# Gated projection of a hybrid decoder trunk: the values of two column slices by seven block products as well, and the gates' weight sums by adding loads

## The chip, the cores and the metric

The kernel runs on one core of one Trainium2 chip. The metric is the device time of one execution, in microseconds (us); the kernel before takes 1935.12 us in the median of three runs (1935.08 to 1935.7). One execution was profiled. In it TensorE (PE) multiplies, VectorE (DVE) and ScalarE (ACT) prepare operands, GpSimd (POOL) and SyncE (SP) issue loads, each on a queue of its own, and 16 DMA engines move the data.

## The reference

A trunk of four residual layers on 256 tokens of width 2048, all float32: a convolution module, a dense MLP, a state-space layer, a dense MLP, then a norm. The change touches the end of the state-space layer, its gated projection:

```
y = jax.nn.gelu(y)                 # (256, 2048)
z = y @ w_glu                      # w_glu: (2048, 4096)
val, gate = jnp.split(z, 2, axis=-1)
x = x + val * jax.nn.sigmoid(gate)
```

Then the next MLP begins: `h = rms_norm(x, mlp_norm[1])`, `a = relu(h @ w_up)`, and so on. All weights come from HBM in float32, and each is used once.

## The kernel before

**Steps and halves.** The program is a list of steps (`self.steps`). A step is 1 MB of weights, 512 rows by 512 columns, which arrives in two halves of 512 KB, tiles of 128x1024. `run_steps` walks through the halves: it loads some steps ahead, splits some halves ahead, and multiplies. A plain step's halves are loaded by SP (`fetch`, L103) into one of six `raw` buffers.

**The split.** float32 is multiplied in three passes. `split` copies a half to a rounded tile `hi` on ACT (L156) and puts the remainder into `lo` on DVE (L163). There are four `hi` and four `lo` buffers, so a half can be split only when PE has done the half four places before it.

**A plain entry.** `mm_t` (L268 to L270) multiplies each half with 12 matmuls of 512 columns: two blocks of 128 rows, two blocks of 128 tokens, three passes. A plain entry is thus 24 matmuls. The activations are `yT`, the transposed output of the state-space part, made in four groups B = 0 to 3 of 512 rows each.

**The projection** (`glu`, from L1578). The outputs are four column slices n of 512 columns, each with values (h = 0) and gates (h = 1). For n = 0 and 1 the rows of groups 0 and 1 are multiplied first, by plain entries, and the partial sums are kept in `st["p"]`, named `part` in the profile. Slice n = 2 follows. Groups 2 and 3 of slices 0 and 1 are then added: the gates by `seven`, the values by four plain entries. Slice 3 is spread among these and ends the stage. While the first entries run, the last groups of the state-space part are finished at set places (`todo`), and loads of its tables (`Wt`, `Mt`, `Vt`) go out on SP's queue.

**Seven products** (`seven`, L745). A 2x2 block of weights B(r, c) (row parity r, column slice c) times a 2x2 block of activations is formed with seven block products instead of eight. A product is 12 matmuls (L759 to L761, accumulators `mp`, `mq`, `mr`), half a plain entry for PE, but it has two halves to split like one. The products' weights are, in order: 1: B(0,0); 2: X = B(0,0)+B(0,1); 3: B(1,1); 4: X, to which B(1,1) has been added; 5: Y = B(0,1)+B(1,1); 6: B(1,0); 7: X, to which B(1,0) has been added too. After each product `take` adds or subtracts the accumulator to one or two 128x512 blocks of `part` on DVE. The combined activations stand in the tile `F`, formed by `forms(2)` and `forms(3)`.

**Two ways to sum weights.** `also` lets DVE add a raw half to a tile `sum` (after `lo`, in `split`). A chain (`add_chain`) loads on POOL's queue: a plain load into `sum` (L129), or an adding load that adds the HBM data to what the tile holds (L123). Tiles `sum` come from a pool of six 512 KB buffers (tag `t4`), shared with temporaries of the stage. Before the change X is summed by DVE and Y, and X's last term, by adding loads.

**What sets the order.** The steps' order is written out by hand at the end of `glu`. Within it a scheduler places the instructions on each engine; every engine and every queue then works in its order.

Of the kernel before, what the change touches and what calls it, by code (L numbers as in the profile page):

```python
# [14 lines left out]
ALU = mybir.AluOpType  # L15
# [6 lines left out]
D = 2048  # L22
# [9 lines left out]
NQ = 4  # L32
# [5 lines left out]
class Trunk:  # L38
# [66 lines left out]
    def load(self, i, half=None):  # L105
        view, shape, _, pre = self.steps[i]
        for kind in self.before_load.pop(i, ()):
            self.table(*kind)
        self.loaded = i + 1
        chain = None  # L110
        if view is None:
            return
        if pre == "x":
            chain, shape = shape, [P, 4, 512]
            if i >= self.widen_from and self.wide is None:
                self.widen()
        nk = shape[1] // 2
        for hf in (0, 1) if half is None else (half,):
            k = slice(hf * nk, hf * nk + nk)
            size = [P, nk] + list(shape[2:])  # L120
            if chain is not None:
                if hf in chain:
                    self.nc.gpsimd.dma_start(out=chain[hf], in_=view[:, k], accum_op=ALU.add)  # L123
                    continue
                raw = chain[hf] = self.sum_tile(size)
            else:
                raw = self.raws[2 * i + hf] = self.w.tile(size, F32, tag="raw", name="raw", bufs=6)
            if chain is not None:
                self.nc.gpsimd.dma_start(out=raw, in_=view[:, k])  # L129
            elif len(shape) == 4:  # L130
                for j in range(shape[2]):
                    self.fetch(raw[:, :, j, :], view[:, k, j, :])
            else:
                self.fetch(raw, view[:, k])
# [607 lines left out]
            self.after(4, lambda: self.square_rstd(ssq))  # L742


    def seven(self, B, A, take, done, start):  # L745

        acc = {}

        def part(i, form, bank, first, *takes):
            def consume(hi, lo, half):
                start()
                if first and half == 0:
                    acc[bank] = self.bank([P, 512], name="m" + bank)
                mm = partial(self.nc.tensor.matmul, acc[bank], skip_group_check=True)
                for j in range(2):
                    F = [A(form, half, j, low) for low in range(2)]
                    mm(lhsT=F[0], rhs=hi[:, j, :], start=first and half == j == 0, stop=False)  # L759
                    mm(lhsT=F[0], rhs=lo[:, j, :], start=False, stop=False)  # L760
                    self.mm_last = mm(lhsT=F[1], rhs=hi[:, j, :], start=False, stop=half == j == 1)  # L761
                if half == 1:
                    with self.tc.high_priority(offset=URGENT):
                        for c, b, sub in takes:
                            take(c, b, sub, acc[bank])
                    if i in done:
                        done[i]()
            return consume
        A11, A22, A12, S1, S2, S3, S4 = range(1, 8)
        add, sub = 0, 1  # L770
        X, Y = {}, {}
        load = self.add_chain

        def plain(b, c, *sums):
            if sums:
                self.also[len(self.steps)] = sums
            self.add(b, [P, 4, 512], c)
        return [lambda: load(B(0, 1), Y),
                lambda: plain(B(0, 0), part(1, A11, "p", True, (0, 0, add)), X, Y),
                lambda: load(None, X, part(2, S1, "r", True, (1, 1, sub))),  # L780
                lambda: plain(B(1, 1), part(3, S4, "r", False, (1, 0, sub)), X, None),
                lambda: load(None, X, part(4, S2, "p", False, (1, 0, sub))),
                lambda: load(B(1, 1), Y, part(5, S3, "p", False, (1, 1, sub))),
                lambda: plain(B(1, 0), part(6, A12, "q", True, (0, 0, add))),
                lambda: load(B(1, 0), X, part(7, A22, "p", False, (0, 1, add)))]

    def mlp(self, layer, last_slice, last_block, hooks=None):
# [131 lines left out]
        if layer == 0:  # L919
# [18 lines left out]
            return down(nsl - 1)  # L938
        self.widen_from = len(self.steps)
        m = [[seven(s, n) for n in (0, 2)] for s in range(nsl)]  # L940
        for k in range(7):
            up(0, k)
# [635 lines left out]
    def glu(self):  # L1578
        w = self.a["ssm_w_glu"][0]
        st = {}  # L1580
# [56 lines left out]
        def out(B):  # L1637
            with self.behind(self.mm_last):
                self.ssm_out(B)
            return self.yt  # L1640

        def local(B):
            with self.behind(self.mm_last):
                self.ssm_local(B)
            return self.mmm

        def carry(B):
            with self.behind(self.mm_last):
                self.ssm_carry(B)
            return self.vmm  # L1650
# [14 lines left out]
        def scale3():  # L1665
            with self.behind(self.lo_ins):
# [5 lines left out]
                (5, 0): (lambda: local(2), scale3), (6, 0): (lambda: front(3),),  # L1672
                (6, 1): (lambda: turn(3), lambda: scan(3)), (7, 1): (lambda: forth(3),), (8, 1): (lambda: states(3),),
                (7, 0): (lambda: carry(2),), (8, 0): (lambda: out(2),), (9, 0): (lambda: local(3),),
                (11, 0): (lambda: carry(3),), (12, 0): (lambda: out(3),), (13, 0): (lambda: forms(2),),
                (13, 1): (lambda: forms(3),)}
        self.before_load = {len(self.steps) + i: t for i, t in ((6, (("W", 3),)), (7, (("M", 2), ("R", 3))), (10, (("V", 2),)),
                                                                (11, (("M", 3),)), (14, (("V", 3),)))}
        self.barrier = len(self.steps)

        order = [(n, B) for n in (0, 1) for B in (0, 1)] + [(2, B) for B in range(NQ)]
        order += [(n, B) for n in (0, 1) for B in (2, 3)] + [(3, B) for B in range(NQ)]

        def forms(B):

# [18 lines left out]
            b, m = ((0, 0), (1, 1), (0, 1))[i - 1]  # L1704
            return self.yT[1][:, 4 * half + 2 * j + m, low, b * P:(b + 1) * P]

        def gates():

            v = w[D // 2:].rearrange("(k two p) c -> two p k c", two=2, p=P)

            def take(c, b, sub, acc):
                c = st["p"][:, c, 1, b]
                self.tt(c, acc, c, ALU.add) if not sub else self.tt(c, c, acc, ALU.subtract)

            def done(n):
                self.nc.scalar.activation(st["p"][:, n, 1], st["p"][:, n, 1], AF.Sigmoid)
                self.glu_out(n, st["p"][:, n, 0], st["p"][:, n, 1])
                self.feed(n, st["ssq"], "mlp1")
            return self.seven(lambda r, c: v[r, :, :, D + c * 512:D + (c + 1) * 512], side, take,
                              {5: lambda: done(1), 7: lambda: done(0)}, lambda: None)  # L1720
        plain = []
        for i, (n, B) in enumerate(order):
            for h in (1, 0):
                def consume(hi, lo, half, n=n, B=B, h=h, i=2 * i + 1 - h):
                    ins = None
                    for fn in todo.pop((i, half), ()):
                        ins = fn() or ins
                    if i == half == 0:
                        st["ssq"] = self.new_ssq()
                    two = n < 2  # L1730
                    first = (B == 0 or two and B == 2) and half == 0
                    last = (B == NQ - 1 or two and B == 1) and half == 1
                    if first:
                        st[h] = self.acc2()
                    k0 = (B % 2) * 4 + half * 2
                    with self.behind(ins) if ins is not None else nullcontext():
                        self.mm_t(st[h], lambda kk: self.yT[B // 2][:, k0 + kk], hi, lo, first, last)
                    if not last:
                        return
                    if B == 1:  # L1740
                        if n == 0 and h == 1:
                            st["p"] = self.blk_tile([P, 2, 2, NB, 512], name="part")
                        self.nc.scalar.activation(st["p"][:, n, h], st[h], AF.Copy)
                    elif two:
                        self.tt(st["p"][:, n, 0], st[0], st["p"][:, n, 0], ALU.add)
                    elif h == 1:
                        st["g"] = self.t4([P, NB, 512], name="sg")
                        self.nc.scalar.activation(st["g"], st[1], AF.Sigmoid)
                    else:
                        if n == 2:  # L1750
                            self.new_hT()
                        self.glu_out(n, st[0], st["g"])
                        self.feed(n, st["ssq"], "mlp1")
                plain.append(partial(self.add_t, w, B * 4, h * D + n * 512, consume, begin if i == 0 and h == 1 else None))
        g = gates()
        a, p = plain[17:24:2], plain[24:]
        for e in (*plain[:15], g[0], plain[15], g[1], a[0], g[2], a[1], g[3], a[2], g[4], a[3], g[5], p[0], g[6], p[1], g[7],
                  *p[2:]):
            e()

    def glu_out(self, n, val, g):
# [97 lines left out]
```

## Time and profile before

| | |
|---|---|
| median of three runs | 1935.12 us (1935.08 to 1935.7) |
| the profiled execution's own time | 1935.06 us |
| its span in the profile | 1933.3 us |
| granted TensorE clock, mean | 0.999 |
| PE busy | 1915.5 us, 99% of the span |
| DVE / ACT / POOL busy | 86% / 58% / 20% |
| DMA | 468 MB, mean 242 GB/s |

Times of the trace are in us from the span's start. The projection's first matmul with `yT` starts at 1060.7, its last product of the gates ends at about 1223, and the next MLP's first matmuls start at 1256. Busy times of an engine add up the durations of its instructions that overlap at their ends, so the pace of an engine is read from the starts of successive instructions. "Landing" of a load is counted from its issue.

### The profile page before, as it was taken

The page shows a single profiled execution, that of the slowest core. Times are in us where ns is not written, and L with a number is a line of the kernel's source. Part 1 is how long each engine was busy: PE and PEld are TensorE (multiplying, and loading weights), DVE is VectorE, ACT ScalarE, POOL GpSimd, SP SyncE. Part 2 cuts the span into 40 slices and gives each one's busy share as a digit, 9 for nine tenths or more (in the row PEclk, how much of TensorE's full clock was granted, in tenths as well). Part 3 has the DMA queues.
Part 4 walks back from the last instruction along what each step waited for, and adds up shares of the span by engine and source line. Part 5 has one row for each costly group of instructions (what it writes and reads, how often), then busy time and mean ns, then how long its engine had stood idle before and what let it go on. Part 6 is the DMA issues. An engine that isn't in the chain of part 4 may idle for free.

```text
span 1933.3 us, 30420 instructions
## 1 busy us (share of the span) xinstructions
PE 1915.5 (99%) x11372; PEld 1641.5 (85%) x11372; DVE 1656.2 (86%) x2246; ACT 1124.9 (58%) x1405; POOL 395.6 (20%) x364
## 2 busy tenths in 40 slices
PE   8999999999999999999999999999999999999998
PEld 8999788888888888888888788888888888888887
DVE  6999798899878898988557869679999999999987
ACT  6444555554465565655545446566666666667664
POOL 3899300001021221213101001001111111111100
PEclk9999999999999999999999999999999999999999
DMA  9667468778788888888898978668998998989984
GB/s 247 186 183 217 124 209 251 220 243 270 251 205 251 238 289 233 280 225 278 280 339 302 337 247 219 195 208 229 260 265 228 266 265 239 260 252 254 247 258 145
DMA packets 338675, 468.45 MB, mean 242 GB/s; under 512 B 16801, under 2 KB 218593, under 8 KB 335169
## 3 DMA queue, kind: packets, MB, share of 16 engines
q1 hardware_dynamic: 296464, 364.69, 59.1%
q0 software_dynamic: 38496, 97.27, 21.5%
q10 hardware_dynamic: 3568, 4.56, 0.8%
q8 instruction: 89, 1.46, 0.3%
q14 instruction: 58, 0.48, 0.1%
HBM read 439.93 MB, written 34.91 MB: 246 GB/s over the span
## 4 chain that ended last, share of the span: by engine, by line
PE 96%; DVE 2%; DMA 1%; issue 0%; ACT 0%; POOL 0%; SPq 0%; POOLq 0%; DVEq 0%; ACTq 0%
PE acc L245 24%; PE acc L248 13%; PE acc L268 7%; PE acc L269 7%; PE acc L270 7%; PE mp L760 4%; PE mp L761 4%; PE mp L759 4%; PE acc L257 3%; PE acc L259 3%; PE acc L258 3%; PE acc L278 2%; PE acc L277 2%; PE acc L279 2%; PE mr L760 2%; PE mr L759 2%
## 5 line engine op out<-in xcount | busy, mean ns | idle before, releaser
L156 ACT ACTIVATE hi<-raw 128x1024 fp32r<-128x1024 f32 x634 | 670.9, 1060 | 622.2 <-PE acc L245 201.4
L163 DVE TENSOR_TENSOR lo<-raw,hi 128x1024 fp32r<-128x1024 f32 x573 | 695.6, 1221 | 184.1 <-ACT hi L156 169.7
L245 PE MATMUL acc<-hT,hi 128*128 128x512 f32 x2048 | 516.6, 392 | 0.1
L245 PEld LDWEIGHTS acc<-hT,hi 128*128 128x128 f32 x2048 | 370.8, 189 | 71.0 <-ACT hi L156 1.7
L248 PEld LDWEIGHTS acc<-hT,lo 128*128 128x128 f32 x2048 | 279.4, 190 | 21.1 <-issue 1.2
L248 PE MATMUL acc<-hT,lo 128*128 128x256 f32 x2048 | 287.0, 282 | 0.0
L156 ACT ACTIVATE hi<-sum 128x1024 fp32r<-128x1024 f32 x152 | 161.4, 1062 | 103.2 <-DVE sum L1025 26.9
L163 DVE TENSOR_TENSOR lo<-sum,hi 128x1024 fp32r<-128x1024 f32 x152 | 185.3, 1219 | 23.9 <-ACT hi L156 14.8
L123 POOL DMA_DIRECT2D sum<-in_mlp_w_down_dram x72 | 87.7, 1222 | 548.8 <-DVE v L1034 310.3
L163 POOL TENSOR_TENSOR lo<-raw,hi 128x1024 fp32r<-128x1024 f32 x60 | 144.0, 2414 | 30.2 <-ACT hi L156 24.1
L257 PE MATMUL acc<-hT,hi 128*128 128x256 f32 x512 | 146.2, 286 | 0.9 <-ACT hi L156 0.9
L259 PE MATMUL acc<-hT,lo 128*128 128x256 f32 x512 | 145.4, 286 | 0.2 <-POOL lo L163 0.2
L258 PE MATMUL acc<-hT,hi 128*128 128x256 f32 x512 | 145.5, 285 | 0.0
L1034 DVE SCALAR_TENSOR_TENSOR cv<-vT,cv 128x256 f32<-128x256 f32 x348 | 141.0, 487 | 2.6 <-ACT cv L587 2.2
L760 PE MATMUL mp<-lo,rT 128*128 128x512 f32 x288 | 112.4, 390 | 0.0
L761 PE MATMUL mp<-hi,rT 128*128 128x512 f32 x288 | 112.2, 390 | 0.0
L759 PE MATMUL mp<-hi,rT 128*128 128x512 f32 x288 | 110.4, 390 | 0.0
L257 PEld LDWEIGHTS acc<-hT,hi 128*128 128x128 f32 x512 | 98.9, 193 | 3.4 <-issue 2.1
L259 PEld LDWEIGHTS acc<-hT,lo 128*128 128x128 f32 x512 | 98.4, 193 | 1.7 <-issue 0.8
L258 PEld LDWEIGHTS acc<-hT,hi 128*128 128x128 f32 x512 | 98.8, 193 | 0.9 <-issue 0.8
L269 PE MATMUL acc<-lo,rT 128*128 128x512 f32 x240 | 93.6, 390 | 0.0
L268 PE MATMUL acc<-hi,rT 128*128 128x512 f32 x240 | 93.6, 391 | 0.0
(359 smaller groups left out, 3247.0 us busy)
## 6 DMA issues: line engine op xcount, KB each, us to landing
raw<-in_mlp_w_up_dram SPq DMA_DIRECT2D x256, 512.0 KB, 6.0
raw<-in_mlp_w_down_dram SPq DMA_DIRECT2D x220, 512.0 KB, 5.7
sum<-in_mlp_w_down_dram POOLq DMA_DIRECT2D x108, 512.0 KB, 7.8
raw<-in_conv_w_in_dram SPq DMA_DIRECT2D x128, 256.0 KB, 3.7
raw<-in_ssm_w_glu_dram SPq DMA_DIRECT2D x62, 512.0 KB, 5.0
raw<-in_conv_w_out_dram SPq DMA_DIRECT2D x32, 512.0 KB, 4.2
Vd<-bv POOLq DMA_DIRECT2D x16, 512.0 KB, 5.6
Md<-Kd POOLq DMA_DIRECT2D x32, 256.0 KB, 7.1
```

Of the source, the lines that this page charges most:

```text
L156: self.nc.scalar.activation(hi, sl, AF.Copy)
L163: ins = eng.tensor_tensor(out=lo, in0=sl, in1=hi.bitcast(F32), op=ALU.subtract)
L245: mm(accs[m], lhsT=hi[:, kk, cs[m]], rhs=xT(k0 + kk), start=first and kk == 0, stop=False)
L248: mm(accs[m][:, 0:T], lhsT=lo[:, kk, cs[m]], rhs=xT(k0 + kk)[:, 0, :], start=False, stop=last and kk == 3)
L257: mm(accs[m], lhsT=hi[:, kk, c], rhs=x[:, 0, :], start=first and kk == 0, stop=False)
L258: mm(accs[m], lhsT=hi[:, kk, c], rhs=x[:, 1, :], start=False, stop=False)
L259: mm(accs[m], lhsT=lo[:, kk, c], rhs=x[:, 0, :], start=False, stop=last and kk == 3)
L268: mm(acc[:, b, :], lhsT=ak[:, 0, t], rhs=hi[:, kk, :], start=first and kk == 0, stop=False)
L269: mm(acc[:, b, :], lhsT=ak[:, 0, t], rhs=lo[:, kk, :], start=False, stop=False)
L759: mm(lhsT=F[0], rhs=hi[:, j, :], start=first and half == j == 0, stop=False)
L760: mm(lhsT=F[0], rhs=lo[:, j, :], start=False, stop=False)
L761: self.mm_last = mm(lhsT=F[1], rhs=hi[:, j, :], start=False, stop=half == j == 1)
```

## The change

- The values' rows of groups 2 and 3 of slices 0 and 1, four plain entries before, become seven products, V1 to V7, by the same function as the gates' G1 to G7 (`second(0)`, `second(1)`). The two DVE additions of 128x1024 that added the plain accumulators to `part` go.
- The values' X is summed by DVE, as the gates' was. The gates' X is now summed by loads alone (`dma`): X and Y are both loaded with B(0,1), then B(0,0) and B(1,1) are added to X, B(1,1) to Y and B(1,0) to X. The blocks that are products of their own are loaded a second time for it.
- The order: slice 2's last entries and slice 3's entries are interleaved with the products. The list of plain entries is now 24 long (0 to 7 slices 0 and 1, 8 to 15 slice 2, 16 to 23 slice 3). P14 means the entry 14 of it. `forms(2)` moves three entries ahead.

```diff
-    def seven(self, B, A, take, done, start):
+    def seven(self, B, A, take, done, start, dma=False):
...
+        def both():
+            load(B(0, 1), X)
+            load(B(0, 1), Y)
+        x1, x2 = ((), ()) if dma else ((X, Y), (X, None))
+        more = lambda b: b if dma else None
+        return [both if dma else lambda: load(B(0, 1), Y),
+                lambda: plain(B(0, 0), part(1, A11, "p", True, (0, 0, add)), *x1),
+                lambda: load(more(B(0, 0)), X, part(2, S1, "r", True, (1, 1, sub))),
+                lambda: plain(B(1, 1), part(3, S4, "r", False, (1, 0, sub)), *x2),
+                lambda: load(more(B(1, 1)), X, part(4, S2, "p", False, (1, 0, sub))),
                 lambda: load(B(1, 1), Y, part(5, S3, "p", False, (1, 1, sub))),
                 lambda: plain(B(1, 0), part(6, A12, "q", True, (0, 0, add))),
                 lambda: load(B(1, 0), X, part(7, A22, "p", False, (0, 1, add)))]
...
-                (11, 0): (lambda: carry(3),), (12, 0): (lambda: out(3),), (13, 0): (lambda: forms(2),),
+                (11, 0): (lambda: carry(3),), (12, 0): (lambda: out(3),), (10, 1): (lambda: forms(2),),
...
-        order = [(n, B) for n in (0, 1) for B in (0, 1)] + [(2, B) for B in range(NQ)]
-        order += [(n, B) for n in (0, 1) for B in (2, 3)] + [(3, B) for B in range(NQ)]
+        order = [(n, B) for n in (0, 1) for B in (0, 1)] + [(n, B) for n in (2, 3) for B in range(NQ)]
...
-                    elif two:
-                        self.tt(st["p"][:, n, 0], st[0], st["p"][:, n, 0], ALU.add)
...
-        g = gates()
-        a, p = plain[17:24:2], plain[24:]
-        for e in (*plain[:15], g[0], plain[15], g[1], a[0], g[2], a[1], g[3], a[2], g[4], a[3], g[5], p[0], g[6], p[1], g[7],
-                  *p[2:]):
+        v, g = second(0), second(1)
+        for e in (*plain[:13], plain[13], v[0], plain[14], v[1], v[2], plain[15], v[3], v[4], plain[16], v[5], v[6],
+                  plain[17], v[7], g[0], g[1], g[2], plain[18], g[3], g[4], plain[19], g[5], plain[20], g[6], g[7],
+                  plain[21], plain[22], plain[23]):
             e()
```

POOL's queue in the projection, whose rows are the loads of `sum` halves. Before, all six of them: `sum_11453` and `sum_11455` are the two halves of the gates' Y, `sum_11598` and `sum_11604` those of their X.

```order
L129 DMA sum_11453<-in_ssm_w_glu_dram 128x2x512
L129 DMA sum_11455<-in_ssm_w_glu_dram 128x2x512
L123 DMA sum_11453<-in_ssm_w_glu_dram 128x2x512
L123 DMA sum_11455<-in_ssm_w_glu_dram 128x2x512
L123 DMA sum_11598<-in_ssm_w_glu_dram 128x2x512
L123 DMA sum_11604<-in_ssm_w_glu_dram 128x2x512
```

After the change there are 18 in this place: six plain and twelve adding. The first four are the values' Y (two plain, two adding), the last two add B(1,0) to the gates' X. Shown are the twelve between: `sum_11556` and `sum_11566` are the values' X, `sum_11818` and `sum_11820` the gates' X, `sum_11844` and `sum_11846` the gates' Y.

```order
L129 DMA sum_11818<-in_ssm_w_glu_dram 128x2x512
L123 DMA sum_11818<-in_ssm_w_glu_dram 128x2x512
L123 DMA sum_11556<-in_ssm_w_glu_dram 128x2x512
L123 DMA sum_11566<-in_ssm_w_glu_dram 128x2x512
L129 DMA sum_11820<-in_ssm_w_glu_dram 128x2x512
L129 DMA sum_11844<-in_ssm_w_glu_dram 128x2x512
L123 DMA sum_11820<-in_ssm_w_glu_dram 128x2x512
L129 DMA sum_11846<-in_ssm_w_glu_dram 128x2x512
L123 DMA sum_11844<-in_ssm_w_glu_dram 128x2x512
L123 DMA sum_11846<-in_ssm_w_glu_dram 128x2x512
L123 DMA sum_11818<-in_ssm_w_glu_dram 128x2x512
L123 DMA sum_11820<-in_ssm_w_glu_dram 128x2x512
```

What moved: the additions to a tile follow its own plain load on one queue, so POOL holds an adding load until the load before it on the same tile has landed, and the two that bring X to X+B(1,1) now stand behind all the others shown.

ACT's splits around the gates' fourth product, in the projection. Before, six halves have been split between the use of X (`sum_11598`, `sum_11604`) for G2 and that for G4, the last two G4's neighbours `raw_11723` and `raw_11725`; DVE has added B(1,1) to X in that time, and no load stands between the two uses.

```order
L156 ACTIVATE hi_11750<-raw_11688 128x1024
L303 ACTIVATE hT_11635<-xt_11666,vecs_229 128x256
L156 ACTIVATE hi_11767<-raw_11723 128x1024
L156 ACTIVATE hi_11788<-raw_11725 128x1024
L156 ACTIVATE hi_11798<-sum_11598 128x1024
L156 ACTIVATE hi_11811<-sum_11604 128x1024
L156 ACTIVATE hi_11828<-raw_11784 128x1024
```

After the change: `sum_11818` and `sum_11820` are split for G2, then the halves of P18 (`raw_11900`, `raw_11902`) and of G3 (`raw_11912`, `raw_11914`), then the two again for G4, each of which waits for its adding load of B(1,1); behind them stand the halves of P19.

```order
L156 ACTIVATE hi_11908<-sum_11818 128x1024
L156 ACTIVATE hi_11916<-sum_11820 128x1024
L156 ACTIVATE hi_11927<-raw_11900 128x1024
L156 ACTIVATE hi_11940<-raw_11902 128x1024
L156 ACTIVATE hi_11951<-raw_11912 128x1024
L156 ACTIVATE hi_11966<-raw_11914 128x1024
L156 ACTIVATE hi_11982<-sum_11818 128x1024
L156 ACTIVATE hi_12000<-sum_11820 128x1024
L156 ACTIVATE hi_12010<-raw_11962 128x1024
L156 ACTIVATE hi_12025<-raw_11964 128x1024
```

What moved: between the two uses of X stand four other halves, where before there were six, and a load on POOL's queue has to land in that time.

More of the change, by code (lines that the diff above doesn't have):

```diff
@@ L777, in plain @@
             self.add(b, [P, 4, 512], c)
[L778 to L782, printed above, removed]
+        def both():
[8 more added lines that the diff above has]
+                lambda: load(more(B(1, 1)), X, part(4, S2, "p", False, (1, 0, sub))),
                 lambda: load(B(1, 1), Y, part(5, S3, "p", False, (1, 1, sub))),
@@ L1705, in side, with second @@
             return self.yT[1][:, 4 * half + 2 * j + m, low, b * P:(b + 1) * P]
-        def gates():
+        def second(h):
             v = w[D // 2:].rearrange("(k two p) c -> two p k c", two=2, p=P)
             def take(c, b, sub, acc):
-                c = st["p"][:, c, 1, b]
+                c = st["p"][:, c, h, b]
                 self.tt(c, acc, c, ALU.add) if not sub else self.tt(c, c, acc, ALU.subtract)
@@ L1718, in done @@
                 self.feed(n, st["ssq"], "mlp1")
-            return self.seven(lambda r, c: v[r, :, :, D + c * 512:D + (c + 1) * 512], side, take,
-                              {5: lambda: done(1), 7: lambda: done(0)}, lambda: None)
+            return self.seven(lambda r, c: v[r, :, :, h * D + c * 512:h * D + (c + 1) * 512], side, take,
+                              {5: lambda: done(1), 7: lambda: done(0)} if h else {}, lambda: None,
+                              h==1)
         plain = []
@@ L1730, in consume @@
                     two = n < 2
-                    first = (B == 0 or two and B == 2) and half == 0
-                    last = (B == NQ - 1 or two and B == 1) and half == 1
+                    first = B == 0 and half == 0
+                    last = B == (1 if two else NQ - 1) and half == 1
                     if first:
```

## The prediction

> **What bounds the kernel now.** I read the page first (span, busy shares, the chain of waits), then the stretches of the projection, then its engines' timelines.
>
> ```profile
> span 1933.3 us, 30420 instructions
> PE 1915.5 (99%) x11372; PEld 1641.5 (85%) x11372; DVE 1656.2 (86%) x2246; ACT 1124.9 (58%) x1405; POOL 395.6 (20%) x364
> PE 96%; DVE 2%; DMA 1%; issue 0%; ACT 0%; POOL 0%; SPq 0%; POOLq 0%; DVEq 0%; ACTq 0%
> ```
>
> PE is busy 99% and holds 96% of the chain: the kernel is as long as its matmuls. Is that so where the change works? The columns are the stretch, its length, busy time (count) of PE, PEld, DVE, ACT, POOL, then PE's clock, DMA share and GB/s.
>
> ```profile
> 1108.00:1256.00 148.00, 147.92 (x839) 122.53 (x840) 109.73 (x115) 80.57 (x98) 6.33 (x6) 1.00 0.74 226
> 1166.00:1210.00 44.00, 44.00 (x199) 36.50 (x199) 39.87 (x40) 27.91 (x32) 4.84 (x4) 1.00 0.87 227
> ```
>
> From 1108 to the next MLP PE has 0.08 us of idle time, at full clock. So every matmul removed there is worth its pace, and there is no stall left to remove. In the 44 us of the gates' products DVE is at 91% and the DMA engines at 87%: these are what a change can run into.
>
> **The matmuls removed.** The pace is the distance of starts; here are the first and last of 25 successive starts on PE, and a row of a product's matmuls:
>
> ```profile
> 1148.36 0.39 PE L268 MATMUL acc<-hi,yT 128*128 128x512 f32 x1
> 1153.80 0.39 PE L268 MATMUL acc<-hi,yT 128*128 128x512 f32 x1
> L760 PE MATMUL mr<-lo,F x8: 389/389/395, 1178.3 to 1188.5; 128*128 128x512 f32 x8
> ```
>
> 24 steps in 5.44 us are 0.227 us each; products' matmuls have the same 389 ns, so the same pace. A plain entry costs PE 5.44 us, a product 2.72. Four plain entries (96 matmuls) become seven products (84): 12 x 0.227 = **2.7 us less**, 0.14%. That is all that can be won, under the 0.2% (3.9 us) that a measurement of this kernel can tell from no change.
>
> **VectorE and ScalarE.** Added: six more halves to split (14 for 8) and seven `take`s of 128x512; removed: two additions of 128x1024. The four DVE sums of weights pass from the gates to the values. Paces and the split's latency:
>
> ```profile
> 1171.37 1.22 DVE L163 TENSOR_TENSOR lo<-raw,hi 128x1024 fp32r<-128x1024 f32 x1
> 1172.50 1.22 DVE L163 TENSOR_TENSOR lo<-sum,hi 128x1024 fp32r<-128x1024 f32 x1
> 1173.63 0.68 DVE L1025 TENSOR_TENSOR part<-mp,part 128x512 f32<-128x512 f32 x1
> 1174.23 1.22 DVE L1025 TENSOR_TENSOR x<-x,sg 128x1024 f32<-128x1024 f32 x1
> 1133.26 1.06 ACT L156 ACTIVATE hi<-raw 128x1024 fp32r<-128x1024 f32 x1 [1.66 <-PE acc L270]
> 1134.35 1.23 DVE L163 TENSOR_TENSOR lo<-raw,hi 128x1024 fp32r<-128x1024 f32 x1 [1.49 <-ACT hi L156]
> ```
>
> DVE takes 1.13 us for 1024 columns and 0.60 for 512: 6 x 1.13 + 7 x 0.60 - 2 x 1.13 = 8.7 us more. ACT gets 6 x 1.0 us more and is at 63% in that stretch. Does DVE's work stay hidden? Let V1 start on PE at T = 0; then PE's nominal starts are V2 2.7, P15 5.4, V3 10.9, V4 13.6, P16 16.3, V5 21.8, V6 24.5, P17 27.2, V7 32.6, G1 35.4, G2 38.1, P18 40.8, G3 46.2, G4 49.0. DVE's densest piece runs from the first `take` (T = 2.7) in its order: take, two `lo` of P15, `lo` and sum, take, `lo` and sum of V3, `lo` of V4, `sg`, `lo` of V4, `lo` of P16. Added up by the paces, P15's first `lo` is done at 4.5 (needed at 5.4), V4's second at 14.1 (needed at 15.0), P16's first at 15.3 (needed at 16.3). The smallest margin is 0.9 us, so I cost it at nothing; if DVE's operations don't close up (1.49 us idle before the row above), it is 1 to 4 us.
>
> `forms(2)`, three entries earlier, falls into DVE's 1.5 us gaps between `lo`s: nothing. After G7 three plain entries (16.3 us) remain before the next MLP instead of six; from the last `take` to the last feature tile of that slice it now takes 14.1 us:
>
> ```profile
> 1223.38 0.68 DVE L1025 TENSOR_TENSOR part<-mp,part 128x512 f32<-128x512 f32 x1
> 1236.64 0.88 DVE L304 SCALAR_TENSOR_TENSOR hT<-xt,vecs,hT 128x256 fp32r<-128x256 f32 x2 [0.15 <-ACT hT L303]
> ```
>
> It fits by 2.2 us; without that cover it would cost what is missing, 1 or 2 us.
>
> **The loads.** SP loses two raw halves. POOL's six become 18, 12 of them adding. What one costs is read from the four adding loads of before (issue, and landing in the order of issue), and from the queues' shares from 1166 to 1210 (q0 is POOL's, q1 SP's):
>
> ```profile
> 1166.04 1.23 POOL L123 DMA_DIRECT2D sum<-in_ssm_w_glu_dram  x1 [51.36 <-DVE sum L1025]
> 1168.83 1.22 POOL L123 DMA_DIRECT2D sum<-in_ssm_w_glu_dram  x1 [1.56 <-DVE sum L1025]
> 1191.61 1.20 POOL L123 DMA_DIRECT2D sum<-in_ssm_w_glu_dram  x1 [21.56 <-DVE lo L163]
> 1193.34 1.20 POOL L123 DMA_DIRECT2D sum<-in_ssm_w_glu_dram  x1 [0.54 <-DVE lo L163]
> DMA to landing us min/median/max: 9.0/9.0/9.0
> DMA to landing us min/median/max: 10.2/10.2/10.2
> DMA to landing us min/median/max: 8.0/8.0/8.0
> DMA to landing us min/median/max: 10.5/10.5/10.5
> q1 hardware_dynamic: 4079, 7.88, 57.5%
> q0 software_dynamic: 1088, 2.10, 28.9%
> ```
>
> An adding load of 512 KB lands about 9.0 us after its issue, and the second of a pair 4.0 and 4.2 us after the first (1179.0 against 1175.0, 1203.8 against 1199.6). Its packets alone hold the 16 engines for 28.9% x 44 / 4 = 3.2 us, a raw half's for 57.5% x 44 / 15 = 1.7 us. A pair of the last MLP (L123) and the plain `sum` loads (L129) there:
>
> ```profile
> L123 POOL DMA_DIRECT2D sum<-in_mlp_w_down_dram x2: 1195/1196/1197, 1619.0 to 1620.3; - x2
> DMA to landing us min/median/max: 6.1/7.3/8.5
> L129 POOL DMA_DIRECT2D sum<-in_mlp_w_down_dram x28: 742/749/752, 1260.2 to 1839.9; - x28
> DMA to landing us min/median/max: 5.2/6.8/8.7
> ```
>
> There the second lands 3.7 us after the first, and a plain load takes 6.8 us. No row shows a train of more than two. So the spacing s in a train is bounded by 3.2 (packets without gaps) and 4.1 (this stage's pairs). I take 3.8: nearest the closest pair, since a full queue has no start-up gaps.
>
> Now POOL's queue as it stands. The values' Y is added to at T = -4.6 and -1.9 (after DVE's sums), landing at 4.4 and 8.2. The gates' first X is loaded by 9.9; its addition waits for that (9.9, lands 18.9). The two for V7 are issued at 12.0 and 14.2 behind V4's `lo`s, landing 22.7 and 26.5 (needed near 30: fine). The gates' second X and first Y go out at 16.5 and 19.3 and land at 28.2 and 29.9. The addition to that X waits for 28.2 and lands at 37.2; behind it stand Y's second load (38.9) and Y's first addition (42.7). Y's second addition waits at the head of the queue until 38.9 and lands at 47.9. Only behind it come the two additions of B(1,1) to X for G4, issued at 40.1 and 41.3: they land at 51.7 and 55.5. Split in 2.3 us (1.06 + 1.23), G4's second half is ready at 57.8. PE wants it at 50.3. ACT's splits for P19 wait behind it in order, so nothing else can fill PE. PE is **7.5 us late**, all of it at G4 (G2's sums are just in time). The same list with s = 3.2 gives 4.5 us, with 4.1 it gives 9.0. What comes after (X for G7, two loads in 19 us) fits.
>
> The sum: 1935.06 (the profiled execution, 0.06 under the median of 1935.12) - 2.7 + 7.5 = **1939.9 us**.
>
> A rule weighs against this step, and a result of its own hangs on it (first rival). The Trainium skill, DMA: Bandwidth & Descriptors, section "Two DMAs through the same engine are not ordered", says that the descriptors of one queue start in order but are pipelined, so that a later one doesn't wait for an earlier one's write. By that, successive adding loads would overlap and the spacing fall below 3.2; the pairs above, 3.7 to 4.2 apart, show little of it.
>
> **The rivals.**
>
> *The loads stay hidden (1932.4 us).* If adding loads overlap so that s is 2.3 or less, each step of 1 us in s being worth 5 us of lateness (9.0 against 4.5 for 0.9), G4 is on time and the 2.7 us are won. For it: PE waits nowhere for these loads in the last MLP, where they come by pairs. Against it: 12 adding loads in some 60 us, not four in 44.
>
> *The 16 engines are short (1943 to 1947 us).* From T = -5 to 47 the loads want 10 x 3.2 (adding) + 18 x 1.7 (14 raw, 4 plain) = 63 us of 52. If the raw halves come late too, the whole excess of 11 us goes to PE in place of the 7.5, and up to 4 us more where the two waits come in turn. It decides once raw halves land more than 13.6 us after issue, since six `raw` and four `hi` buffers let them go out ten halves (of 1.36 us, in products) ahead. For it: the sum above. Against it: the 7 us for P19 and P20 in it aren't due by then, and a raw half's median is 5.0 us now:
>
> ```profile
> raw<-in_ssm_w_glu_dram SPq DMA_DIRECT2D x16, 512.0 KB, 5.0
> ```
>
> *VectorE is the bound (1933 to 1936 us).* The loads are in time, but DVE loses its 0.9 us margin at P15 or P16; 1 to 4 us, against 2.7 won.
>
> That the matmuls aren't saved can be excluded: the order on PE has 12 fewer.
>
> **How the numbers follow.** POOL's train sets the end: 0.58, its own range 1936.9 (s = 3.2) to 1943 (s = 4.1 gives 1941.4, a little more where the train meets more raw loads than the pairs did). It passes 0.2% at 6.6 us of lateness, s = 3.6; I put 0.43 above that and 0.15 below. Hidden loads: 0.23, within 0.2% but for 0.03 where the stage also gains elsewhere. Engines short: 0.11, slower. VectorE: 0.08, within. So slower 0.54, within 0.2% 0.43, faster 0.03. The range, 1932 to 1946, takes in the hidden loads and half of the engines' case.
>
> **What would show it.** PE idle between G2 and P19 with ACT's `hi<-sum` as the releaser, and behind it the landing of an L123 load; spacings of 3.5 to 4.2 us in POOL's landings; PE's 12 matmuls fewer; no idle time at V1 to V7. Wrong it would be if PE stayed without gaps from V1 to G7 (then 1932.4), or if it waited for `lo` of a raw half, with DVE (VectorE) or SP's loads (engines) behind it.

## The result, and the profile after

The change made the kernel slower: 1942.62 us (median of six, 1941.48 to 1944.67) against 1935.47 us for the kernel before, measured beside it (1935.08 to 1935.7). The ratio is 1.0039, with a 95% interval of 1.0026 to 1.0052. The forecast was 1939.9 us, so the direction and the place were right; the time came out 2.7 us above it, and the loss against the kernel before was 7.2 us, where 4.8 were forecast. The profiled execution took 1941.86 us.

The page after: the same three lines as those shown of before.

```profile
span 1940.0 us, 30442 instructions
PE 1916.3 (99%) x11360; PEld 1640.0 (85%) x11360; DVE 1664.6 (86%) x2257; ACT 1130.2 (58%) x1411; POOL 407.7 (21%) x376
PE 93%; DMA 3%; DVE 2%; issue 1%; POOL 1%; ACT 0%; SPq 0%; POOLq 0%; DVEq 0%; ACTq 0%
```

PE has its 12 matmuls fewer, but its share of the chain fell from 96% to 93% and DMA's rose from 1% to 3%. The stretches of the projection after (length, busy time and count of PE, PEld, DVE, ACT and POOL, PE's clock, DMA share, GB/s):

```profile
1108.00:1264.00 156.00, 150.60 (x834) 122.49 (x834) 119.26 (x128) 86.93 (x105) 19.08 (x18) 0.98 0.86 252
1163.85:1214.14 50.29, 50.21 (x225) 41.11 (x223) 40.55 (x43) 30.64 (x35) 13.69 (x13) 1.00 1.04 280
1214.14:1227.08 12.94, 7.97 (x21) 5.26 (x20) 6.87 (x7) 6.02 (x6) 2.39 (x2) 0.74 0.98 214
```

From V1's first matmul (1163.85, the prediction's T = 0) to the end of G3 PE is busy without a gap worth naming. In the 13 us behind that it is busy for 8, and its granted clock is 0.74. That is where the loss lies. PE's timeline there (start, duration, line, operation, and in brackets the idle time and its releaser), first G3's last matmul, then G4 and the start of P19:

```profile
1213.91 0.39 PE L761 MATMUL mr<-hi,F 128*128 128x512 f32 x1
1217.43 0.49 PE L759 MATMUL mp<-hi,F 128*128 128x512 f32 x1 [3.13 <-ACT hi L156]
1218.69 0.50 PE L760 MATMUL mp<-lo,F 128*128 128x512 f32 x1 [0.76 <-DVE lo L163]
...
1219.90 0.63 PE L761 MATMUL mp<-hi,F 128*128 128x512 f32 x1
1221.45 0.80 PE L759 MATMUL mp<-hi,F 128*128 128x512 f32 x1 [0.92 <-ACT hi L156]
1222.40 0.80 PE L268 MATMUL acc<-hi,yT 128*128 128x512 f32 x1 [0.15 <-ACT hi L156]
...
1226.38 0.40 PE L269 MATMUL acc<-lo,yT 128*128 128x512 f32 x1
...
1227.08 0.39 PE L269 MATMUL acc<-lo,yT 128*128 128x512 f32 x1
```

G4 would have started at 1214.14, and the twentieth matmul from there on, the one at 1227.08, at 1214.14 + 19 x 0.227 = 1218.45. So 8.6 us are lost here. The four waits, counted from start to start over the usual 0.227 us (3.29, 1.03, 1.32, 0.72), make 6.4 us of it. The rest, 2.2 us, is pace: the nine steps from 1222.40 to 1226.38 take 3.98 us, where they would take 2.04. The split is not sharp, since the last two of the four waits hold a slow matmul each.

Who let PE wait is read on ACT and POOL. ACT's timeline, the splits of G4's two halves of X and of P19's first raw halves:

```profile
1216.33 1.06 ACT L156 ACTIVATE hi<-sum 128x1024 fp32r<-128x1024 f32 x1 [8.86 <-DMA sum<-in_ssm_w_glu_dram]
1220.34 1.06 ACT L156 ACTIVATE hi<-sum 128x1024 fp32r<-128x1024 f32 x1 [2.96 <-DMA sum<-in_ssm_w_glu_dram]
1221.31 1.99 ACT L156 ACTIVATE hi<-raw 128x1024 fp32r<-128x1024 f32 x2
```

ACT itself stood idle for 8.86 and 2.96 us until adding loads had landed, and P19's halves stood behind them in its order. POOL's timeline of the issues before that (L123 adds, L129 is plain):

```profile
1192.57 1.23 POOL L123 DMA_DIRECT2D sum<-in_ssm_w_glu_dram  x1 [7.00 <-DMA sum<-in_ssm_w_glu_dram]
1193.32 1.24 POOL L129 DMA_DIRECT2D sum<-in_ssm_w_glu_dram  x1
1194.51 1.29 POOL L123 DMA_DIRECT2D sum<-in_ssm_w_glu_dram  x1
1203.57 3.67 POOL L123 DMA_DIRECT2D sum<-in_ssm_w_glu_dram  x3 [7.78 <-DMA sum<-in_ssm_w_glu_dram]
```

The `x3` are the gates' second addition to Y and the two additions of B(1,1) to X for G4. The first of them could not be issued before the plain load to its own tile (1193.32) had landed, and both of X's stood behind it. They landed 7.8, 11.9 and 15.2 us after their issues, at 1211.4, 1216.2 and 1220.2.

The account, by the first and last starts of the plain matmuls on `yT`, before and then after:

```profile
L268 PE MATMUL acc<-hi,yT x224: 388/389/504, 1060.7 to 1255.1; 128*128 128x512 f32 x112
L270 PE MATMUL acc<-hi,yT x224: 387/389/481, 1061.7 to 1255.6; 128*128 128x512 f32 x112
```

```profile
L268 PE MATMUL acc<-hi,yT x192: 387/389/796, 1061.1 to 1262.1; 128*128 128x512 f32 x192
L270 PE MATMUL acc<-hi,yT x192: 387/389/632, 1062.1 to 1262.5; 128*128 128x512 f32 x192
```

From 1060.7 to 1255.6 before and from 1061.1 to 1262.5 after, the projection got 6.5 us longer. The terms are -2.7 (12 matmuls), +8.6 (G4) and +0.24 (P15, below), together 6.1; 0.4 us is not accounted for. Outside the projection the two differ by 0.2 us.

### The profile page after: what moved, and what is told of

Its sections match the earlier page's. It is cut to its first block, busy times and chain, and to the rows that moved or that the text cites. A ratio compares the mean times of both kernels' runs of the same rounds, so it can differ in the third digit from the quotient of the medians.

```text
span 1940.0 us, 30442 instructions
## 1 busy us (share of the span) xinstructions
PE 1916.3 (99%) x11360; PEld 1640.0 (85%) x11360; DVE 1664.6 (86%) x2257; ACT 1130.2 (58%) x1411; POOL 407.7 (21%) x376
## 4 chain that ended last, share of the span: by engine, by line
PE 93%; DMA 3%; DVE 2%; issue 1%; POOL 1%; ACT 0%; SPq 0%; POOLq 0%; DVEq 0%; ACTq 0%
PE acc L245 24%; PE acc L248 13%; PE acc L268 6%; PE acc L269 6%; PE acc L270 6%; PE mp L761 4%; PE mp L760 4%; PE mp L759 4%; PE acc L257 3%; PE acc L259 3%; PE acc L258 3%; PE acc L278 2%; PE acc L277 2%; PE acc L279 2%; PE mr L760 2%; PE mr L759 2%
## 5 line engine op out<-in xcount | busy, mean ns | idle before, releaser
L156 ACT ACTIVATE hi<-sum 128x1024 fp32r<-128x1024 f32 x160 | 170.0, 1063 | 124.3 <-DVE sum L1030 33.2
L163 DVE TENSOR_TENSOR lo<-sum,hi 128x1024 fp32r<-128x1024 f32 x160 | 194.9, 1219 | 35.1 <-ACT hi L156 25.7
L123 POOL DMA_DIRECT2D sum<-in_mlp_w_down_dram x72 | 87.6, 1222 | 548.0 <-DVE v L1039 309.4
```

The source lines that it names most:

```text
L156: self.nc.scalar.activation(hi, sl, AF.Copy)
L163: ins = eng.tensor_tensor(out=lo, in0=sl, in1=hi.bitcast(F32), op=ALU.subtract)
```

## The experiments

The theory: the gates' train of adding loads on POOL's queue brings X + B(1,1) too late for G4, and nothing else in the change costs time. The rivals: VectorE is the bound; the 16 engines are short of time for the bytes; the matmuls behind the wait are slow for a reason of their own.

### The gates' weight sums on VectorE

```
-                              h==1)
+                              False)
```

Both second halves of the contraction still go by seven products, but no sum is made by a load that VectorE made before. That is six loads fewer on POOL's queue, two plain and four adding (the expectation counts eight).

> The values go by seven products as in the change, but the gates' X is summed by VectorE again (four additions of 128x1024 more on VectorE, eight loads fewer on GpSimd's queue). Theory (the train of adding loads makes G4 late): no wait at G4 for a load; the 2.7 us are won, less 0.2 to 1 us where VectorE is just late: 1933 to 1934 us. Rival (VectorE is the bound): 4 x 1.13 = 4.5 us more on VectorE in the gates' products come out as PE waiting for lo: 1936 to 1938 us. Rival (the values' products themselves cost the time): 1939 us or more.

1933.44 us (1932.98 to 1934.94), against 1935.63 for the kernel before in the same comparison; ratio 0.9989, interval 0.998 to 0.9998. All groups of waits on PE from 1100 to 1300 (us in total, times, longest), and then the 44 us from 1166, in the columns of the stretches above:

```profile
PE xtr L1487 <- ACT X L1473: 0.3, 1, 0.3
```

```profile
1166.00:1210.00 44.00, 43.92 (x197) 35.73 (x196) 41.58 (x44) 28.99 (x35) 5.53 (x5) 1.00 0.89 234
```

The only wait left lies in the state-space part ahead of the stage, and the whole loss is gone although VectorE has more to do: it is busy 41.58 us of these 44, against 39.87 before. So VectorE is not the bound, and the values' part of the change pays for itself. This version beats both kernels: it wins 2.2 of the 2.7 us that the saved matmuls are worth.

### The same loads, without adding

```
+                    if 16 <= i - self.glu_from <= 40:
+                        self.nc.gpsimd.dma_start(out=chain[hf], in_=view[:, k])
+                    else:
                         self.nc.gpsimd.dma_start(..., accum_op=ALU.add)
```

Twelve adding loads become plain ones to the same tiles with the same waits; the additions of weights are left out of the computation.

> As the change, but the 12 adding loads of the projection are plain loads into the same tiles, with the same waits and bytes from HBM (the kernel leaves out these additions of weights). Theory: plain loads land some 6.8 us after issue and 1.7 to 2 us apart, G4's two land at T = 44 and 45 instead of 52.5 and 56.5, in time: 1932.5 to 1934 us. Rival (bytes from HBM or the waits on the queue alone, whatever the load does): G4 is still 4 us late or more: 1938 us or more.

1933.3 us (1932.71 to 1935.09), ratio 0.9989, interval 0.998 to 0.9998. ACT's timeline at G4's two halves, which no longer wait for a load:

```profile
1210.62 1.06 ACT L159 ACTIVATE hi<-sum 128x1024 fp32r<-128x1024 f32 x1 [1.43 <-PE acc L273]
1213.34 1.06 ACT L159 ACTIVATE hi<-sum 128x1024 fp32r<-128x1024 f32 x1 [1.66 <-PE acc L273]
```

The bytes, the number of loads and the waits for landings that POOL's queue has are those of the change. What costs time is that these loads add. POOL's queue from 1160 to 1215 (packets, MB, share of 16 engines' time), in the change and then in this run:

```profile
q0 software_dynamic: 3051, 6.88, 59.1%
```

```profile
q0 software_dynamic: 2019, 7.35, 38.9%
```

A MB took 59.1% x 55 / 6.88 = 4.7 us of the 16 engines in the change and 2.9 us here.

### G4's place: P19 ahead of it

```
-  plain[17], v[7], g[0], g[1], g[2], plain[18], g[3], g[4], plain[19], g[5], ...
+  plain[17], v[7], g[0], g[1], g[2], plain[18], g[3], plain[19], g[4], g[5], ...
```

> As the change, but the plain entry P19 stands ahead of G4 instead of behind it, so that G4 is due 5.44 us later; the loads and their order on GpSimd's queue stay. Theory: G4's wait of 7.0 us (for its sums, at full clock) shrinks by 5.4 us to 1.6 us, and PE's clock isn't lowered behind it: 1934 to 1936 us. Rival (the 16 engines are short): P19's raw halves are wanted earlier and come late, the wait only changes its name: 1939 us or more.

1938.27 us (1937.13 to 1941.69), ratio 1.0014, interval 1.0005 to 1.0023: better than the change by 4.4 us, but not the 1934 to 1936 that the theory gave. ACT's splits of G4's halves, and then two of the groups of waits on PE from 1100 to 1300:

```profile
1215.75 1.06 ACT L156 ACTIVATE hi<-sum 128x1024 fp32r<-128x1024 f32 x1 [3.11 <-DMA sum<-in_ssm_w_glu_dram]
1219.83 2.96 ACT L156 ACTIVATE hi<-sum 128x1024 fp32r<-128x1024 f32 x3 [3.02 <-DMA sum<-in_ssm_w_glu_dram]
```

```profile
PE mp L760 <- DVE lo L163: 1.5, 2, 0.8
PE acc L269 <- DVE lo L163: 1.3, 1, 1.3
```

X's halves land when they did, and G4's own wait shrinks to about 1 us, as the theory has it. The miss lies in what it left out: the splits of the entries behind G4 stand behind G4's on ACT and VectorE, and PE now waits for them in small pieces (1.3 us for `lo` of the plain entry behind). Moving the product hides a late load only as far as the splits behind it are not late too.

### Y's loads behind X's

```
+        def held():
+            self.held.add(len(self.steps))
+            load(B(1, 1), Y, part(5, S3, "p", False, (1, 1, sub)))
...
+                    with self.behind(self.added) if i in self.held else nullcontext():
+                        self.added = self.nc.gpsimd.dma_start(..., accum_op=ALU.add)
```

The two additions of B(1,1) to Y, which G5 needs, go behind the two to X, which G4 needs. The order on PE, ACT and VectorE is that of the change.

> The change with one thing moved: the two adding loads of Y+B(1,1) for the gates, which the fifth product needs, are issued behind the two of X+B(1,1), which the fourth needs. In the change they stand ahead of them, POOL waits for Y to land before it issues the second of them (until 1203.57), and each takes its 4.0 us of the train. Order on PE, ACT and VectorE, bytes and instructions are the same. Theory (place in the train): X's halves are issued at some 1202 and 1204 and land some 8 us earlier than in the change, at 1208 to 1212; the fourth product finds them there; Y lands at 1216 to 1220, ahead of the fifth product; 1933 to 1934.5 us. Rival (the engines are short of time for these bytes, whatever the order): as many us are lost, at the fourth product or, moved on, at the fifth or at plain entries; 1938 us or more.

1934.84 us (1934.15 to 1936.19), against 1935.28 for the kernel before; ratio 0.9999, interval 0.999 to 1.0007. This is 7.8 us under the change, from the order of four loads. POOL's issues, and then ACT's splits of the two halves:

```profile
1201.65 1.21 POOL L125 DMA_DIRECT2D sum<-in_ssm_w_glu_dram  x1 [8.58 <-DVE lo L165]
1203.38 3.67 POOL L125 DMA_DIRECT2D sum<-in_ssm_w_glu_dram  x3 [0.53 <-DVE lo L165]
```

```profile
1209.51 1.06 ACT L158 ACTIVATE hi<-sum 128x1024 fp32r<-128x1024 f32 x1 [2.40 <-DMA sum<-in_ssm_w_glu_dram]
1214.28 1.06 ACT L158 ACTIVATE hi<-sum 128x1024 fp32r<-128x1024 f32 x1 [3.71 <-DMA sum<-in_ssm_w_glu_dram]
```

X's additions now wait only until G2's `lo` has read the tile, and G4 gets its halves 6.8 and 6.1 us earlier; 0.9 us of waits is left on PE there. So the train's order, not its length alone, made the change slow, and a shortage of the engines by itself does not explain it, since the same bytes move. The gain of the 12 matmuls is not reached as in the two runs above.

### Fewer raw bytes beside the train

```
+                cut = self.glu_from is not None and 16 <= i - self.glu_from <= 40
+                if cut:
+                    k = slice(hf * nk, hf * nk + 1)
+                    self.raws[2 * i + hf] = raw[:, 0:1].broadcast_to([P, nk, 512])
+                    raw = raw[:, 0:1]
                 self.fetch(raw, view[:, k])
```

Is the train slow because it shares the 16 engines with SP's raw loads? Here SP loads half the bytes of the plain entries.

> The change with the weights of the projection's plain entries from the third quarter of its loads on half loaded: SP's raw loads fetch only the first of the two blocks of rows in each half, and both splits read that block twice, so the second block's weights are left out of the computation. POOL's adding loads, the order and all instructions on PE, ACT and VectorE stay. If the 4.0 us between landings of adding loads comes from sharing the 16 engines with SP's loads, they land some 3.2 us apart here, the fourth product's wait falls by 4 to 7 us, and the time is 1934 to 1938.5 us. If an adding load takes 4.0 us of its queue by itself, the spacing stays at 3.9 to 4.1 and the time at 1941 to 1943 us.

1935.37 us, but the ten runs range from 1934.41 to 1941.77, and the profiled one (1940.23) still has 2.8 us of waits for G4's `hi`. Neither expectation fits. A second kernel takes a quarter of the bytes (the second half of an entry reads the block of the first, by `self.raws[2 * i + 1] = self.raws[2 * i]`).

> As the run with half of SP's raw bytes, but a quarter of them: for the projection's plain entries from the third quarter of its loads on, one block of 128 rows is loaded and read for all four of an entry, so three of four blocks of these weights are left out of the computation. The adding loads stay as in the change. That run gave no clear answer: its median fell to 1935.4 us, its runs ranged from 1934.4 to 1941.8, and in its profile the last three landings of the train were no nearer to one another than in the change. If the train is slow because it shares the 16 engines with SP's loads, it comes still earlier here: the fourth product's wait is gone in all runs, 1932.5 to 1934.5 us, and the last landings are 3.3 us apart or less. If an adding load holds its queue for some 4 us by itself, the last landings stay 3.7 us apart or more, a wait at the fourth product is left in some runs, and the time is 1935 to 1940 us.

1934.37 us (1933.49 to 1936.64), ratio 0.9998, interval 0.9989 to 1.0008. POOL's issue that headed the `x3` in the change, then ACT's splits of X's halves, then SP's queue between the landings of the three loads that were the `x3` there (1206.68 to 1209.80, and 1209.80 to 1213.77):

```profile
1199.19 1.21 POOL L124 DMA_DIRECT2D sum<-in_ssm_w_glu_dram  x1 [6.79 <-DMA sum<-in_ssm_w_glu_dram]
```

```profile
1209.91 1.06 ACT L165 ACTIVATE hi<-sum 128x1024 fp32r<-128x1024 f32 x1 [3.24 <-DMA sum<-in_ssm_w_glu_dram]
1213.88 1.06 ACT L165 ACTIVATE hi<-sum 128x1024 fp32r<-128x1024 f32 x1 [2.91 <-DMA sum<-in_ssm_w_glu_dram]
```

```profile
q1 hardware_dynamic: 22, 0.05, 4.3%
q1 hardware_dynamic: 265, 0.48, 34.8%
```

The two halves still land 3.97 us apart. But X's first half lands 3.12 us behind Y's second, where it was 4.84 us in the change, and in these 3.12 us SP's queue held only 4.3% of the engines' time (39.5% in the change). So one spacing shrank with the raw traffic, and the next one, with SP at 34.8% against 66.0% in the change, did not. Whether 4 us is the queue's own or comes from sharing is not settled by this run.

X's first half lands 5.6 us earlier than in the change, counted from each kernel's first adding load (1158.86 and 1159.65). 3.6 us of it is the head of the train: the plain loads ahead of it land sooner, and the first addition held behind one goes out at 1199.19 instead of 1203.57. The rest is mostly the shorter spacing. The time of 1934.37 us lies in the range of the first expectation, the last spacing in that of the second.

For the half-sized run this leaves open why its runs spread so far: two of ten took over 1940 us, one of them the profiled one, and two more over 1936.5.

### The wait filled with matmuls

```
+                if dma and i == 4:
+                    self.keep_warm((28, 18)[half], self.mm_last)
```

Does the slow pace behind the wait cost anything by itself? Matmuls of 128x128 that nobody reads fill the wait.

> As the change, with 28 and 18 dummy matmuls of 128x128 on PE ahead of G4's two halves, inside its wait (some 5 us of 0.11 us each); no operand of them is waited for. Theory of the clock (1.6 of the 8.6 us lost at G4 come from matmuls at half clock behind PE's idle time): the granted clock stays 1.00 and 1 to 1.6 us come back: 1941 us against 1942.6. Rival (the clock falls for another reason, or the whole 8.6 us are the loads): no change, 1942 to 1943.5 us.

1943.21 us (1942.94 to 1943.43): no gain. PE's timeline, with the two rows of fillers (L235) and the starts of G4's halves:

```profile
1213.81 6.41 PE L235 MATMUL warm<-ident 128*128 128x128 f32 x56
1219.97 0.48 PE L761 MATMUL mp<-hi,F 128*128 128x512 f32 x1
...
1221.45 4.18 PE L235 MATMUL warm<-ident 128*128 128x128 f32 x36
1225.38 0.48 PE L761 MATMUL mp<-hi,F 128*128 128x512 f32 x1
```

Each filler is two passes on PE (56 records for 28), 0.23 us. They held G4 back: it starts 2.5 us later than in the change and its second half 3.9 us later, while the weights landed as before. The clock stayed at 1.00 from 1212 to 1230, and the fillers took what it gave. So fewer of them:

```
-                    self.keep_warm((28, 18)[half], self.mm_last)
+                    self.keep_warm((14, 6)[half], self.mm_last)
```

> The change with 14 and 6 matmuls of 128x128 that nobody reads put ahead of the two halves of the fourth product, so that they fill the wait of TensorE but end before the weights come. Theory (some 1.6 us of the loss are matmuls at half the granted clock behind the wait): the clock stays above 0.95 from 1213 to 1230, the matmuls behind the wait start 0.23 us apart instead of 0.43, and the time is 1940.7 to 1941.6 us. Rival (the slow matmuls cost nothing, since the weights set the pace there): 1942.3 to 1943 us.

1940.77 us (1938.68 to 1942.77, five runs), 1.85 us under the change, about what the slow pace was counted at, but the two ranges overlap. In the profiled run, the slowest of the five, P19's matmuls behind the wait start 0.23 us apart; ahead of them the clock still fell for four of G4's, so the expected 0.95 throughout did not come, and G4's second half, held back by its fillers, starts 1.4 us after its `hi` is there. This speaks for the pace as a cost of its own of 1 to 2 us, but with ranges that overlap it is not shown.

### The gates' sums by loads alone, the values plain

The kernel before, with the sums of the gates' weights by adding loads (`self.seven(..., True)`), the rest as before.

> The kernel before with one part of the change alone: the gates' weight sums all by adding loads (8 adding loads, 12 on POOL's queue in all); the values stay plain and the order of entries is that of the kernel before, so PE does the 12 matmuls that the change saves and has two plain entries and two products, some 16 us more, between the second and the fourth product of the gates. Theory (the loads cost time only because they come too late for the fourth product): they come in time here, no wait on PE from them, 1934.5 to 1936.5 us, not told from before. Rival (adding loads cost time by themselves, by slowing raw loads or the splits): 1938 us or more, with waits on PE at other entries.

1945.74 us (1945.47 to 1945.95), ratio 1.0054, interval 1.0039 to 1.007: the slowest of all, and a miss of the theory. It has no wait at a product. Of the waits on PE from 1100 to 1300 the largest group; then POOL's first adding loads; then the landing times of the state-space part's 1 MB tables (`Vt`) in this run, and last the same before:

```profile
PE mv L1562 <- DMA Vt<-Vd: 7.8, 2, 5.2
```

```profile
1123.08 2.52 POOL L123 DMA_DIRECT2D sum<-in_ssm_w_glu_dram  x2
```

```profile
DMA to landing us min/median/max: 7.5/11.5/17.3
```

```profile
DMA to landing us min/median/max: 5.7/6.9/7.8
```

In the order of before, POOL is free to fetch the gates' X and Y some 40 us earlier. Its loads meet the tables of the state-space part, which then land up to 17.3 us after issue, and PE waits for them. Is this the adding, too? The same kernel with the eight additions left out:

> The run with the gates' sums alone by adding loads, with the additions of these eight loads left out (plain loads of the same bytes with the same waits, so the sums are missing from the computation). There the loads fell on the stretch in which 1 MB tables of the state-space part come in, these landed 15.7 us after issue instead of 6.9, and TensorE waited 7.8 us for them. If it is the adding that crowds the tables out, they land within 10 us here, TensorE waits under 1 us for them, and the time is 1934.5 to 1936 us. If it is the place of these bytes, added or not, the tables still land over 12 us after issue and the time is 1940 us or more.

1941.83 us (1940.72 to 1943.15), ratio 1.0031, interval 1.002 to 1.0042. The wait, and then the landing times:

```profile
PE mv L1566 <- DMA Vt<-Vd: 3.4, 2, 1.9
```

```profile
DMA to landing us min/median/max: 7.7/9.8/12.4
```

Neither expectation fits fully: plain loads at this place cost 6.4 us over before, and adding 3.9 us more. Here it is mostly the place of the bytes; in the change it was the adding. The change, which takes the gates' second half later, avoids this loss.

## Why the prediction was right, and where it was short

**PE's 12 matmuls** were saved: 11360 for 11372, and without the train's wait the kernel is 2.2 to 2.3 us faster (the first two experiments) of the 2.7 worked out.

**VectorE at nothing** was right for VectorE. The one small wait that came, at P15, has another source. PE's second matmul of P15 comes 0.47 us after the first instead of 0.23, where it waits for the split. The rows are PE's, then VectorE's with the split, then ScalarE's ahead of it:

```profile
1169.29 0.39 PE L268 MATMUL acc<-hi,yT 128*128 128x512 f32 x1
1169.76 0.50 PE L269 MATMUL acc<-lo,yT 128*128 128x512 f32 x1
1168.47 3.50 DVE L163 TENSOR_TENSOR lo<-raw,hi 128x1024 fp32r<-128x1024 f32 x3 [1.02 <-ACT hi L156]
1165.18 1.28 ACT L1751 ACT_TABLE_LOAD   x1
1166.47 1.03 ACT L1751 ACTIVATE sg<-acc 128x1024 f32<-128x1024 f32 x1
```

VectorE had stood idle for 1.02 us until P15's `hi` was there, and ScalarE came to that `hi` only at 1167.39, behind a table load and the sigmoid of slice 2's gates. The prediction followed VectorE's order but took ScalarE by its total alone (63% busy). The wait is 0.24 us, and with more work for VectorE (gates' sums on it) nothing more was lost. **`forms(2)` and the tail behind G7** cost nothing: no wait stands there.

**The train on POOL's queue** was read rightly from the order. The list gave landings for Y's second addition and for G4's two at T = 47.9, 51.7 and 55.5, 3.8 us apart; they came at T = 47.5, 52.4 and 56.4, 4.8 and 4.0 us apart. So the spacing was too short both times, and the bound of 4.1 from this stage's pairs was the better of the two ends. The pair in the last MLP, which the prediction took as nearest to a full queue, misled it. The first rival needed 2.3 us or less; the adding loads of the train landed no closer than 3.8 us in the change. The Trainium skill, DMA: Bandwidth & Descriptors, section "Two DMAs through the same engine are not ordered", has the descriptors of a queue pipelined. The trace agrees in part. The three loads of the `x3` overlap: they were issued within 1.5 us, each took 7.8 us or more to land, and the next one landed 4.8 or 4.0 us after it. That is too little overlap to hide them.

**The lateness of 7.5 us** is the term that was mis-sized: it measured 8.6 us. Errors partly cancel in it, and that it came so near is in part luck. The halves landed 0.7 and 0.9 us later than listed. PE's nominal times left out eight transposes (L299, one row of 1.03 us at 1183.54) and P15's 0.24, so G4 was due at T = 50.3 and not 49.0, which made the wait itself smaller (6.4 us). And no term stood for PE's clock: behind the wait nine steps took 3.98 us instead of 2.04, and with the slower pace ahead of them that adds 2.2. This term is missing from the working. The 1.1 us of lateness, P15's 0.24 and the 0.6 us that stayed unexplained or lie outside the projection bring the forecast to the profiled execution; the median lies another 0.8 us above that.

**The rivals.** "The loads stay hidden" and "VectorE is the bound" fell with the result. "The 16 engines are short" fell as stated: the DMA share was 1.04 from T = 0 to 50, yet raw halves were never what PE waited for. It has a grain of truth: with less raw traffic the train's plain loads came in earlier, and one of its two last spacings fell from 4.8 to 3.1 us. What the prediction did not consider is that the train's own order could be changed, and that this alone takes the loss away.

## What to carry to other kernels

Moving additions to the loading queue frees an engine that may not be the bound, and puts them one behind another: price a train by the spacing of landings (here 3.8 to 4.8 us per 512 KB), follow it in the order of issue to the one consumer that is due first, and put that consumer's loads ahead. A load that waits at the head of such a queue for an earlier one to land holds up all behind it, whoever needs them. When waits on PE of some 4 us in all, close together, are forecast, add a term for the slower pace behind them (here some 2 us). Follow each engine's order, not only its busy share: ScalarE was late at P15 although it was busy for only 61% of the stretch.

## What the runs showed of the hardware that was not expected

Neighbouring adding loads of 512 KB in the train up to G4 landed 3.8 to 4.8 us apart in the change, and 3.1 and 4.0 us apart at its end beside a quarter of SP's bytes for plain entries. Plain loads at the same places kept up with PE.

After 3.3 us without work and shorter gaps PE's pace fell from 0.227 to some 0.43 us per matmul; the granted clock was 0.50 from 1219.51 to 1226.33. The Trainium skill, TensorE: Matmul & The Clock Gate, section "What's actually happening", says that the clock is halved after an idle window of about 3.4 us and full again after as long a busy one; these rows agree roughly, with a mean granted clock of 0.74 over the 13 us. The half-sized run does not agree: counted in the same way, its gaps on PE at G4 were 1.8, 1.0 and 1.3 us, and the clock was halved all the same, as this row of its profile shows (the columns as above).

```profile
1217.82:1224.65 6.83, 5.50 (x13) 3.98 (x13) 5.55 (x6) 4.97 (x5) 1.33 (x2) 0.50 0.71 110
```

So gaps well under 3.4 us can be enough when they come close together. With P19 ahead of G4, gaps of 1.0, 0.3 and 1.6 us were not: the clock stayed at 1.00 from 1218 to 1230.

1 MB table loads went from 6.9 to 11.5 us (median) when six loads of another queue, four of them adding, were put beside them, and PE waited 7.8 us for them; with the six loads plain it was 9.8 us and 3.4 us.
